# Spilled split weight parts, nine operand pages and x chunks in other tiles, in a decoder trunk on one core

## The chip, the core and the metric

The kernel runs on one core of a Trainium2 chip. The metric is the device time of one execution in microseconds (us), the median of several runs. The engines named below are PE (TensorE, the matrix products; PEld are its weight loads), ACT (ScalarE), DVE (VectorE), POOL (GpSimd) and SP (SyncE, which issues nearly all DMA transfers here).

## The reference, cut to what matters

One layer over 2048 positions of width 1024, in float32. Two mixers share one input product (w_in has 3584 columns, which are 28 blocks of 128): a gated linear recurrence of 1024 channels and a short convolution of 512 channels. Then an output product, a gated feed-forward with a convolution, and norms.

```
h = rms_norm(x, norm1_g[l])
z = jnp.einsum('bsd,de->bse', h, w_in[l])
lru_x, lru_gate, sc_b, sc_c, sc_x = jnp.split(z, splits, axis=-1)
lru_x = causal_dwconv(lru_x, lru_conv_w[l]) + lru_conv_b[l]
y_lru = rg_lru(lru_x, lru_wa[l], lru_ba[l], lru_wx[l], lru_bx[l], lru_lambda[l]) \
    * jax.nn.gelu(lru_gate)
y_sc = sc_b * causal_dwconv(sc_c * sc_x, sc_conv_w[l])
y_mix = jnp.concatenate([y_lru, y_sc], axis=-1)
x = x + jnp.einsum('bse,ed->bsd', y_mix, w_out[l])
h = rms_norm(x, norm2_g[l])
u = causal_dwconv(jnp.einsum('bsd,df->bsf', h, w_up[l]), ffn_conv_w[l])
gate, up = jnp.split(u, 2, axis=-1)
x = x + jnp.einsum('bsf,fd->bsd', jax.nn.gelu(gate) * up, w_down[l])
return rms_norm(x, final_g)
```

`rg_lru` forms r and i = sigmoid of two block-diagonal products (the gates), a = exp(-8 r softplus(-lambda)), and scans h[t] = a h[t-1] + sqrt(1 - a^2) i x.

## The kernel before

**Arithmetic.** x is held as its transpose: 8 chunks of 128 partitions by positions. Each float32 operand is split in two: ACT copies it rounded ("hi", L214), DVE subtracts to get the rest ("lo", L215). A product is then three matmuls: hi by hi, hi by lo, lo by hi. A name wh_ or xh is a hi part, wl_ or xl (as an operand) a lo part.

**Stages.** Positions go in two halves of 1024. The first half's input product (0 to 524 us of the profiled execution) takes the 28 blocks one by one, in the order 0, 8, 1, 9, 20, 24, 21, 25, 16, 17, 2, 10, 3, 11, 4, 12, 5, 13, 6, 14, 7, 15, 22, 26, 23, 27, 18, 19; a block is 48 matmuls of 128x512 (L277). Blocks c and 8 + c make recurrent unit c (the input and its gate), 16 to 27 the short convolution. Beside the products runs the tail of each unit: evacuation of PSUM, convolution (L336, L338), the split of its result (xch, xcl) as the operand of the gate products (L373), eight sigmoids (L384), Exp, Tanh, Square and Sqrt (L389 to L393), the scan (L397), Gelu (L400), and the stores of y. Then come the output product's sweeps of that half (524 to 640 us, L967), the second half's input product (640 to 1010 us, L673), its sweeps (to 1176 us), and the feed-forward's up and down products of both halves (to the end).

**The second half.** Its input product goes by pairs of blocks: 14 pairs, each a 2 by 2 problem done in seven products (Strassen-Winograd) of 12 matmuls. Its weight operands are the quarters W11 and W12 (halves of block a of the pair), W22 (of block b), and the sums S1 to S4 of quarters. S1 to S3 are added by DVE in the first half (`pair_sums`, L261) and spilled to DRAM (`si_d`); in the second half `in_weights` (L808) loads two raw tiles for a pair, splits seven operands and adds S4. The steps of a pair are: `begin` (W11), `middle` (S2, then W12 between, then S3), `fourth` (W22), `sum1` (S1) and `end` (S4). The name zxin is the PSUM tile that W11, S2, S3 and W22 add up in one after the other; ACT copies it out in between (L684): g0, g1 to one tile (xlin, prin or sbin), n1 and n0 to another (soin). The tail of the recurrent pair before stands in the step behind `fourth`.

**What sets the order.** PE, SP and POOL run in the order in which the code is written. ACT and DVE are ordered by a scheduler, by the priorities the code gives (weight splits have a raised one) and by when it reckons operands ready. Each engine runs its row in order. SP's row is strict: a transfer that waits for a tile holds all behind it. `defer(n, ...)` notes a store, and `tick()`, called once for each block, issues it n calls later.

**Tiles.** The pools are: "act", 28 pages of 4 KB a partition; "tmp", 7 pages; "w" and "v", 5 each (weights' hi and lo, in turn); "wr", 4 raw weight tiles; "a" and "b" of the pool `ub`, two wide tiles each (`big`). A load into a tile waits for the last reader of what was there. In the first half the eight x chunks of the second half (`xs`, loaded by L1039) are squared on the way for the second half's norm, one after each unit; they take "act" pages, which the tails use as well.

Of the kernel before, what the change touches and what calls it, by code (L numbers as in the profile page):

```python
# [60 lines left out]
}  # L61
PAIR_OF = {o: (PAIRS.index(p), i) for p, ab in BLOCKS.items() for i, o in enumerate(ab)}

TERMS = [("W11", "B11"), ("S2", "T2"), ("S3", "T3"), ("W22", "T4"), ("S1", "T1"), ("S4", "B22"), ("W12", "B21")]

SUMS = [("S1", "W21", "W22"), ("S3", "W21", "W11"), ("S2", "W11", "S1"), ("S4", "W12", "S2")]

# [12 lines left out]
def block_kernel(  # L80
# [44 lines left out]
    si_d = [dr.tile([P, 3, NB], F32, name=f"si_d{i}") for i in range(len(PAIRS))]  # L125
# [117 lines left out]

    raw_of = {}

    def load_weights(o, name, gate=None):
        tick()
        raw_of[o] = raw_tile(f"wr_{name}")
        out = next(load_parts(w_in[o], name, 1, gate, raw_of[o]))
        i, _ = PAIR_OF[o]  # L250
# [124 lines left out]

    def lru_scan(c, half, cv, g, *gates, home=None, sign=1.0):
        n = f"{half}_{c}"
        r, i = (flat((home or act)(f"{x}{n}")) for x in "ri")
        a = big(f"a{n}", c % 2)[:, :T] if home else flat(act(f"a{n}"))
        with tc.high_priority(offset=HP):  # L380
            for k, (rows, ps) in enumerate(zip(HALVES, gates)):
                for b, p in enumerate(ps):
                    for dst, o, at in ((r, O_BA, k), (i, O_BX, 1 - k)):
                        nc.scalar.activation(  # L384
                            dst[rows, blk(b)], p[HALVES[at], :], AF.Sigmoid, bias=col(o + c)[rows, :]
                        )
        nc.vector.tensor_tensor(i, i, cv, ALU.mult)
        m = cv
        nc.scalar.activation(a, r, AF.Exp, scale=nc8[:, c : c + 1])  # L389
        nc.scalar.activation(m, r, AF.Tanh, scale=c8[:, c : c + 1])  # L390
# [6 lines left out]
        nc.vector.tensor_tensor_scan(h, a, i, init, ALU.mult, ALU.add)  # L397
# [4 lines left out]
        nc.vector.tensor_tensor(y, g, h, ALU.mult)  # L402
        return y
# [77 lines left out]
    def in_phase(half, acc, between):  # L481
# [22 lines left out]
            x_square(half, k, acc, xs[k])  # L504
        for _ in loads[2]:
            pass
        for c in range(2):
            load_gate(c, raws[2 * c])
        parts = mean_split(acc, f"a{half}")
# [91 lines left out]
    def x1_prep(k, rs):  # L601
        return operands(f"x_{k}", k, lambda kk: xT[kk, :, T:S], O_G1, rs)

    def operands(name, k, src, gain, rs):
        a = big(f"ha{name}", 0)[:, :T]
        b = big(f"hb{name}", 0)[:, :T]
# [55 lines left out]
    class Pair:  # L662
# [27 lines left out]
        def spread(self):  # L690
            self.open()
            ps = {w: pst(f"z{w}{self.name}") for w, _ in TERMS}
            for k in range(4):
                for w, x in TERMS:
                    self.run(ps[w], w, x, True, True, (k,))
            (g0, g1), (n0, n1) = self.g, self.n
            self.x = ps["W11"]
            self.copy(g0)
# [10 lines left out]
                    nc.vector.tensor_tensor(dst, ps[w], src, ALU.add)  # L709
            self.second_done()  # L710
            self.first_done()

        def begin(self):
            self.open()
# [13 lines left out]
        def middle(self, between):  # L728
            self.run(self.x, "S2", "T2", False, False)
            self.copy(self.g[1])  # L730
            between()
            self.run(self.x, "S3", "T3", False, False)
            self.copy(self.n[1])
            self.add(self.n[1], self.c)

# [70 lines left out]
            cur = nxt  # L806
            between(j)

    def in_weights(i):
        a, b = BLOCKS[PAIRS[i]]  # L810
        one, other = raw_tile(f"wra_in{i}"), raw_tile(f"wrb_in{i}")
        nc.sync.dma_start(one[:, 0, :], w_in[a][:, :NB])
        nc.sync.dma_start(one[:, 1:3, :], si_d[i][:, 1:3, :])
        nc.sync.dma_start(other[:, 0, :], w_in[a][:, NB:])
        nc.sync.dma_start(other[:, 1, :], w_in[b][:, NB:])
        nc.sync.dma_start(other[:, 2, :], si_d[i][:, 0, :])
        tick()
        out = {}

        def operand(name, src):  # L820
            w = page(f"w{name}_in{i}", "v" if i == 0 and name in ("W22", "S4") else "w", 5)
            split(w[:, 0, :], w[:, 1, :], src)
            out[name] = (w[:, 0, :], w[:, 1, :])

        operand("W11", one[:, 0, :])
        operand("S1", one[:, 1, :])
        operand("S2", one[:, 2, :])
        nc.vector.tensor_tensor(one[:, 2, :], one[:, 2, :], other[:, 0, :], ALU.add)
        operand("W12", other[:, 0, :])
        operand("S3", other[:, 2, :])  # L830
        operand("W22", other[:, 1, :])
        operand("S4", one[:, 2, :])
        return out

    def vpage(name):
        return page(name, "v", 5)
# [1 line left out]
    class InPair(Pair):  # L838
# [5 lines left out]
        def open(self):  # L844
# [5 lines left out]
                self.first = with_halo(f"pr{n}", 2, 1, p_halo[:, c, :], c % 2, nc.vector)  # L850
                self.g = halves(self.first, 2)
            else:
                self.first = flat(tmp(f"sb{n}"))
# [10 lines left out]
    def in_blocks(hs, start):  # L864
        half = 1
        gates = {}
        sv = {}
        wts = [in_weights(0), in_weights(1)]
        state = {"gw": None}

        def load_gates(q):
# [4 lines left out]
        def finish(pair):  # L876
            n = UNITS.index(("L" if pair.kind == "L" else "S", pair.unit))
            if pair.kind == "L":
                c = pair.unit
                xc, cv = lru_conv_of(c, half, pair.first, vpage)  # L880

                def gated():
                    if c % 4 == 0:
                        load_gates(c // 4)
                    g = state["gw"][:, c % 4, :]
                    return lru_gates(c, half, xc, (g[:, :P], g[:, P:]))

                def scanned(pss):
                    y = lru_scan(c, half, cv, pair.other, *pss, home=tmp, sign=-1.0)
                    keep_y(half, n, y, (1, 1))  # L890

                gates[pair.name] = (gated, scanned)
# [14 lines left out]
        cur = InPair(0, hs, wts[0])  # L907
        last = None
        for j in range(len(PAIRS)):
            if j + 2 < len(PAIRS):  # L910
                wts.append(in_weights(j + 2))
            else:
                tick()
            nxt = InPair(j + 1, hs, wts[j + 1]) if j + 1 < len(PAIRS) else None
            if j == 0:
                cur.spread()
                nxt.begin()
            elif nxt is None:
                cur.middle(cur.sum1)
                cur.second()  # L920
                cur.fourth()
            else:
                cur.middle(cur.second)
                nxt.begin()
# [6 lines left out]
            if nxt is not None and j + 2 < len(PAIRS):  # L931
                nxt.sum1()
            if j > 0:
                cur.end()
# [92 lines left out]
    def beside_first(n):  # L1027
# [7 lines left out]
                nc.scalar.activation(t, t, AF.Square)  # L1035
                nc.vector.tensor_tensor(ss1[1], ss1[1], t, ALU.add)
        if n < KC:
            t = x1_raw[n] = flat(act(f"xs{n}"))
            nc.sync.dma_start(t, xT[n, :, T:S])  # L1039
# [258 lines left out]
```

## Time and profile before

| what | us |
|---|---|
| median of 3 runs (lowest, highest) | 2548.32 (2544.07, 2548.89) |
| the profiled execution, its own time | 2548.74 |
| its span in the trace | 2545.9 |
| PE busy, share of the span | 2275.8, 89% |
| DVE busy | 1812.3, 71% |
| ACT busy | 1233.6, 48% |
| first half's input product | 0 to 524 |
| sweeps, first half | 524 to 640 |
| second half's input product | 640 to 1010 |

The profiled execution stands at the median of the runs. What lies around its span is 2.84 us. The page's section 2 shows the span in 40 slices of 63.6 us, with the busy tenths of each engine, the granted TensorE clock and the DMA rate:

```profile
PE   8676547799989677899999999999999999999998
PEclk9787868899999889899999999999999999999999
GB/s 186 168 137 57 62 116 126 45 320 284 186 161 186 153 145 97 278 270 91 116 108 88 118 106 87 269 213 222 238 112 87 118 106 87 121 105 300 280 193 179
```

PE is under nine tenths busy in the first eight slices and in slices 12 to 16, and its clock is lower there.

### The profile page before, as it was taken

The numbers are of one execution on the slowest core, as the hardware profiler recorded it, in microseconds if no ns is written. First come the engines' busy times: TensorE is split into PE (matmuls) and PEld (weight loads), VectorE is DVE, ScalarE is ACT, GpSimd is POOL, SyncE is SP. The second block draws the span as 40 slices with busy tenths as digits, with TensorE's granted clock in tenths as the row PEclk, the third lists the DMA queues.
The fourth block names the chain that finished last, engine by engine and source line by source line (L and its number), as shares of the span: only waits on it lengthen the run. The fifth ranks groups of instructions, "written<-read, shape, count | busy, mean of one in ns | idle before, by whom it ended". The sixth has DMA issues, their size and how long they took to land.

```text
span 2545.9 us, 26290 instructions
## 1 busy us (share of the span) xinstructions
PE 2275.8 (89%) x9814; PEld 1854.2 (73%) x9814; DVE 1812.3 (71%) x2108; ACT 1233.6 (48%) x1427; POOL 136.2 (5%) x187
## 2 busy tenths in 40 slices
PE   8676547799989677899999999999999999999998
PEld 6455436678767555677888888888888888888886
DVE  8444436589676556698888788867788788787656
ACT  6513345245656765354554454544445454444343
POOL 0000000000000000000111111000001001000000
PEclk9787868899999889899999999999999999999999
DMA  6551133198656553772332332766632332338765
GB/s 186 168 137 57 62 116 126 45 320 284 186 161 186 153 145 97 278 270 91 116 108 88 118 106 87 269 213 222 238 112 87 118 106 87 121 105 300 280 193 179
DMA packets 160048, 402.41 MB, mean 158 GB/s; under 512 B 15472, under 2 KB 19184, under 8 KB 159344
## 3 DMA queue, kind: packets, MB, share of 16 engines
q1 hardware_dynamic: 149984, 381.86, 43.5%
q0 software_dynamic: 9792, 18.88, 4.6%
q8 instruction: 76, 1.25, 0.2%
q14 instruction: 52, 0.43, 0.1%
q10 hardware_dynamic: 144, 0.00, 0.0%
HBM read 301.07 MB, written 137.36 MB: 172 GB/s over the span
## 4 chain that ended last, share of the span: by engine, by line
PE 76%; DVE 10%; ACT 8%; issue 3%; DMA 2%; SPq 0%; DVEq 0%; ACTq 0%
PE zx L673 20%; PE zin_b L277 11%; PE zc L673 10%; PE dx L967 10%; PE dy L967 8%; PE za L673 5%; PE ox L967 4%; PE zxin L673 4%; PE oy L967 2%; DVE cv L338 2%; ACT r L384 1%; ACT i L384 1%; PE zcin L673 1%; PE zS L673 1%; DVE r L397 1%
## 5 line engine op out<-in xcount | busy, mean ns | idle before, releaser
L277 PE MATMUL zin_b<-xh,wh_in 128*128 128x512 f32 x448 | 148.8, 415 | 145.9 <-ACT wh_in L214 145.9
L277 PEld LDWEIGHTS zin_b<-xh,wh_in 128*128 128x128 f32 x448 | 89.6, 202 | 169.2 <-ACT wh_in L214 149.7
L215 DVE TENSOR_TENSOR fl_d<-wrf_d,fh_d 128x1024 fp32r<-128x1024 f32 x84 | 102.8, 1223 | 123.0 <-ACT fh_d L214 120.5
L214 ACT ACTIVATE fh_d<-wrf_d 128x1024 fp32r<-128x1024 f32 x84 | 89.0, 1060 | 206.2 <-PE dy L967 84.7
L277 PE MATMUL zin_b<-xh,wl_in 128*128 128x512 f32 x448 | 146.2, 409 | 11.6 <-DVE wl_in L215 11.6
L215 DVE TENSOR_TENSOR wla_up<-wra_up,wha_up 128x1024 fp32r<-128x1024 f32 x48 | 58.8, 1225 | 132.8 <-ACT wha_up L214 132.8
L967 PE MATMUL dx<-fh_d,wh_d 128*128 128x512 f32 x384 | 149.4, 389 | 0.0
L967 PE MATMUL dx<-fl_d,wh_d 128*128 128x512 f32 x384 | 149.4, 389 | 0.0
L967 PE MATMUL dx<-fh_d,wl_d 128*128 128x512 f32 x384 | 149.4, 389 | 0.0
L277 PE MATMUL zin_b<-xl,wh_in 128*128 128x512 f32 x448 | 146.1, 408 | 0.2
L338 DVE SCALAR_TENSOR_TENSOR cu<-un,prm,cu 128x1024 f32<-128x1024 f32 x96 | 122.6, 1277 | 4.4 <-ACT cu L334 4.3
L338 DVE SCALAR_TENSOR_TENSOR cg<-ug,prm,cg 128x1024 f32<-128x1024 f32 x96 | 122.7, 1278 | 0.3
L673 PE MATMUL zc<-hhB,whd_up 128*128 128x512 f32 x368 | 120.7, 389 | 0.0
L673 PE MATMUL zx<-ht,whc_up 128*128 128x512 f32 x368 | 113.3, 389 | 0.0
L277 PEld LDWEIGHTS zin_b<-xh,wl_in 128*128 128x128 f32 x448 | 88.1, 198 | 34.1 <-DVE wl_in L215 15.6
L967 PE MATMUL dy<-fh_d,wh_d 128*128 128x512 f32 x288 | 112.0, 389 | 0.0
L967 PE MATMUL dy<-fl_d,wh_d 128*128 128x512 f32 x288 | 112.0, 389 | 0.0
L967 PE MATMUL dy<-fh_d,wl_d 128*128 128x512 f32 x288 | 112.0, 389 | 0.0
L684 ACT ACTIVATE ug<-zx 128x512 f32<-128x512 f32 x92 | 55.0, 598 | 114.8 <-PE zx L673 114.7
L215 DVE TENSOR_TENSOR wl_d<-wrw_d,wh_d 128x1024 fp32r<-128x1024 f32 x84 | 102.3, 1219 | 11.3 <-ACT wh_d L214 10.0
L277 PEld LDWEIGHTS zin_b<-xl,wh_in 128*128 128x128 f32 x448 | 89.2, 200 | 21.0 <-DVE xl L460 1.4
L214 ACT ACTIVATE wh_d<-wrw_d 128x1024 fp32r<-128x1024 f32 x84 | 88.0, 1048 | 22.2 <-DMA wrw_d<-sd_d_S 7.4
(439 smaller groups left out, 6393.5 us busy)
## 6 DMA issues: line engine op xcount, KB each, us to landing
wra_up<-in_w_up SPq DMA_DIRECT2D x48, 512.0 KB, 4.6
wrb_up<-in_w_up SPq DMA_DIRECT2D x48, 512.0 KB, 5.3
f_d_T<-cg SPq DMA_DIRECT2D x96, 256.0 KB, 2.5
wrw_d<-sd_d_S SPq DMA_DIRECT2D x48, 512.0 KB, 4.5
wrf_d<-f_d_T SPq DMA_DIRECT2D x48, 512.0 KB, 4.2
f_d_B<-cu SPq DMA_DIRECT2D x72, 256.0 KB, 2.4
wrw_d<-in_w_down SPq DMA_DIRECT2D x36, 512.0 KB, 4.6
wrf_d<-f_d_B SPq DMA_DIRECT2D x36, 512.0 KB, 3.4
```

The source lines that it names most:

```text
L214: nc.scalar.activation(r32(hi), src, AF.Copy)
L215: nc.vector.tensor_tensor(r32(lo), src, hi, ALU.subtract)
L277: nc.tensor.matmul(ps[t], r32(a), r32(b[:, blk(t)]), start=(first and i == 0), stop=(last and i == 2))
L338: nc.vector.scalar_tensor_tensor(dst, src[:, k : k + T], col(o_w + k), dst, ALU.mult, ALU.add)
L384: nc.scalar.activation(dst[rows, blk(b)], p[HALVES[at], :], AF.Sigmoid, bias=col(o + c)[rows, :])
L397: nc.vector.tensor_tensor_scan(h, a, i, init, ALU.mult, ALU.add)
L673: nc.tensor.matmul(ps, r32(p[:, s]), r32(self.hs[k][x][o]), start=f and i == 0, stop=l and i == 2, skip_group_check=True,)
L684: nc.scalar.activation(dst, self.x, AF.Copy)
L967: nc.tensor.matmul(ps[m], r32(p), r32(x[:, k, :]), start=first and i == 0 and n == 0, stop=(last or not on_x) and i == ni - 1 and n == 2, ...
```

## The change

There are three parts.

- *Spilling.* In the first half `keep_weights` stores hi and lo of W11, W12 and W22 to a new DRAM tile `sw_d`, two ticks after the block's split; `pair_sums` also adds S4, and `si_d` has room for it. SP has 997 rows instead of 913.
- *The second half.* `in_weight` loads one operand at a time: W11, W12, W22 from `sw_d` into a "w" page, without a split; S1 to S4 from `si_d` into a raw tile that is split in place. Nine operands are loaded up front, then seven a step in the order of their use. The stores that are due (`tick`) now go ahead of a step's loads. The tile `so` is taken later (`open_second`), `sb` and the scan's r come from "v" pages, and gate weights are loaded when a pair is finished. The last pair runs like the others.
- *x chunks.* `xs` takes a wide tile of side n % 2 instead of an "act" page, and the first operand of the residual (`x1_prep(0, ...)`) has its second tile on side "b".

```diff
-TERMS = [("W11", "B11"), ("S2", "T2"), ("S3", "T3"), ("W22", "T4"), ("S1", "T1"), ("S4", "B22"), ("W12", "B21")]
+TERMS = [("W11", "B11"), ("S1", "T1"), ("S2", "T2"), ("S3", "T3"), ("W22", "T4"), ("S4", "B22"), ("W12", "B21")]
...
+    def keep_weights(o, hl):
+        i, b = PAIR_OF[o]
+        for n, t in enumerate(hl):
+            t = t.rearrange("p (a b) -> p a b", a=2)
+            if b:
+                defer(2, sw_d[i][:, 2, n, :], t[:, 1, :])
+            else:
+                defer(2, sw_d[i][:, 0:2, n, :], t)
...
+                (ra, 1, ra[:, 1, :], ra[:, 0, :]),
...
-        defer(2, si_d[i][:, 2, :], ra[:, 0, :])
+        defer(2, si_d[i][:, 2:4, :], ra[:, 0:2, :])
...
-        r, i = (flat((home or act)(f"{x}{n}")) for x in "ri")
+        r, i = (flat(p(f"{x}{n}")) for p, x in zip(home or (act, act), "ri"))
...
+    def in_weight(i, op):
+        n = f"w{op}_in{i}"
+        if op in KEPT:
+            t = page(n, "w", 5)
+            nc.sync.dma_start(t, sw_d[i][:, KEPT.index(op)])
+            return t[:, 0, :], t[:, 1, :]
+        t = raw_tile(n)
+        nc.sync.dma_start(t[:, 2, :], si_d[i][:, SPILLED.index(op), :])
+        split(t[:, 0, :], t[:, 1, :], t[:, 2, :])
+        return t[:, 0, :], t[:, 1, :]
...
-            self.other = flat(tmp(f"so{n}"))
+
+        def open_second(self):
+            self.other = flat(tmp(f"so{self.name}"))
...
-        wts = [in_weights(0), in_weights(1)]
+        load(*((0, w) for w, _ in TERMS), (1, "W11"), (1, "S1"))
...
-            if j + 2 < len(PAIRS):
-                wts.append(in_weights(j + 2))
-            else:
-                tick()
+            tick()
+            load(
+                (j + 1, "S2"),
+                (j + 1, "W12"),
+                (j + 1, "S3"),
+                (j + 2, "W11"),
+                (j + 1, "W22"),
+                (j + 2, "S1"),
+                (j + 1, "S4"),
+            )
...
-            t = x1_raw[n] = flat(act(f"xs{n}"))
+            t = x1_raw[n] = big(f"xs{n}", n % 2)[:, :T]
...
-            hx.append(x1_prep(0, ss1[1]))
+            hx.append(x1_prep(0, ss1[1], 1))
```

How the rows of the engines move, at three places. First ACT in the first half, at unit 3 (r_3, a_3, cv_3 are its gate, decay and root; wh_in_12, wh_in_5, wh_in_13 and wh_in_6 are the hi copies of these blocks). Before:

```order
L389 ACTIVATE a_3_1649<-r_3_1647,nc_81 128x1024
L390 ACTIVATE cv_3_1452<-r_3_1647,c_80 128x1024
L1035 ACTIVATE xs_1675<-xs_1675 128x1024
L391 ACTIVATE r_3_1647<-a_3_1649 128x1024
L393 ACT_TABLE_LOAD
L393 ACTIVATE cv_3_1452<-cv_3_1452 128x1024
L214 ACTIVATE wh_in_12_1685<-wr_in_12_1684 128x1024
L214 ACTIVATE wh_in_5_1748<-wr_in_5_1747 128x1024
```

And after:

```order
L217 ACTIVATE wh_in_12_1734<-wr_in_12_1733 128x1024
L217 ACTIVATE wh_in_5_1800<-wr_in_5_1799 128x1024
L403 ACT_TABLE_LOAD
L403 ACTIVATE a_3_1696<-r_3_1694,nc_81 128x1024
L404 ACTIVATE cv_3_1494<-r_3_1694,c_80 128x1024
L1054 ACTIVATE xs_1913<-xs_1913 128x1024
L405 ACTIVATE r_3_1694<-a_3_1696 128x1024
L407 ACT_TABLE_LOAD
L407 ACTIVATE cv_3_1494<-cv_3_1494 128x1024
L414 ACT_TABLE_LOAD
L414 ACTIVATE g_4_1792<-g_4_1792 128x1024
L217 ACTIVATE gw_5_1806<-wr_in_5_1799 128x128
```

The split of block 12 moved from behind the root of unit 3 to ahead of its exponential. In the rows that follow, the split of block 13 moved from behind the root of unit 4 to ahead of that unit's sigmoids.

The second place is ACT at the first unit, where block 20's split stood. Before, it was behind the whole tail of unit 0 (eight sigmoids, which are r_0 and i_0, are left out here); the piece from the last of the tail on is:

```order
L389 ACTIVATE a_0_736<-r_0_734,nc_81 128x1024
L390 ACTIVATE cv_0_595<-r_0_734,c_80 128x1024
L400 ACT_TABLE_LOAD
L400 ACTIVATE g_1_731<-g_1_731 128x1024
L391 ACTIVATE r_0_734<-a_0_736 128x1024
L393 ACT_TABLE_LOAD
L393 ACTIVATE cv_0_595<-cv_0_595 128x1024
L214 ACTIVATE wh_in_20_766<-wr_in_20_765 128x1024
```

And after, ahead of the sigmoids:

```order
L414 ACTIVATE g_0_651<-g_0_651 128x1024
L217 ACTIVATE wh_in_20_788<-wr_in_20_787 128x1024
L217 ACTIVATE xch_1_743<-cv_1_738 128x1024
L1054 ACTIVATE xs_886<-xs_886 128x1024
L398 ACT_TABLE_LOAD
L398 ACTIVATE r_0_750<-zr_0_b_717,prm 64x512
```

The split moved past the whole tail of unit 0.

The third place is SP's row in the second half, at one step (wra_in and wrb_in are raw weight tiles, wS_in and wW_in operands, y_d the stores of y, yc and soin the results of a unit's tail). Before:

```order
L812 DMA wra_in_4955<-in_w_in 128x512
L813 DMA wra_in_4955<-si_d_258 128x1024
L814 DMA wrb_in_4956<-in_w_in 128x512
L815 DMA wrb_in_4956<-in_w_in 128x512
L816 DMA wrb_in_4956<-si_d_258 128x512
L211 DMA y_d_B_1_109<-soin_4563 128x512
L211 DMA y_d_T_1_118<-yc_4_4914 128x512
```

And after:

```order
L214 DMA y_d_B_1_109<-soin_4717 128x512
L214 DMA y_d_T_1_118<-yc_4_4918 128x512
L837 DMA wS_in_4961<-si_d_257 128x512
L834 DMA wW_in_4965<-sw_d_271 128x1024
L837 DMA wS_in_4967<-si_d_257 128x512
L834 DMA wW_in_4971<-sw_d_272 128x1024
L834 DMA wW_in_4973<-sw_d_271 128x1024
L837 DMA wS_in_4975<-si_d_258 128x512
L837 DMA wS_in_4979<-si_d_257 128x512
```

The stores of y moved from behind a step's loads to ahead of them, and five loads became seven.

More of the change, by code (lines that the diff above doesn't have):

```diff
@@ L62 @@
 PAIR_OF = {o: (PAIRS.index(p), i) for p, ab in BLOCKS.items() for i, o in enumerate(ab)}
[L64 removed]
+TERMS = [("W11", "B11"), ("S1", "T1"), ("S2", "T2"), ("S3", "T3"), ("W22", "T4"), ("S4", "B22"), ("W12", "B21")]
+KEPT = ["W11", "W12", "W22"]
+SPILLED = ["S3", "S1", "S2", "S4"]
 SUMS = [("S1", "W21", "W22"), ("S3", "W21", "W11"), ("S2", "W11", "S1"), ("S4", "W12", "S2")]
@@ L124, in block_kernel @@
     sd_d = blocks("sd_d", S_OPS, NI)
-    si_d = [dr.tile([P, 3, NB], F32, name=f"si_d{i}") for i in range(len(PAIRS))]
+    si_d = [dr.tile([P, 4, NB], F32, name=f"si_d{i}") for i in range(len(PAIRS))]
+    sw_d = [dr.tile([P, 3, 2, NB], F32, name=f"sw_d{i}") for i in range(len(PAIRS))]
     sg_d = dr.tile([2, P, NLRU // 2, 2 * P], F32, name="sg_d")
@@ L249, in load_weights @@
         out = next(load_parts(w_in[o], name, 1, gate, raw_of[o]))
+        keep_weights(o, out)
         i, _ = PAIR_OF[o]
@@ L506, in in_phase @@
             pass
+        for o, w in zip((0, NLRU, 1), wts):
+            keep_weights(o, w)
         for c in range(2):
@@ L599, in h_prep, with x1_prep, operands @@
         return operands(f"{half}_{k}", k, lambda kk: x2_d[half][kk // 2][kk % 2], O_G2, rs)
-    def x1_prep(k, rs):
-        return operands(f"x_{k}", k, lambda kk: xT[kk, :, T:S], O_G1, rs)
-    def operands(name, k, src, gain, rs):
+    def x1_prep(k, rs, side=0):
+        return operands(f"x_{k}", k, lambda kk: xT[kk, :, T:S], O_G1, rs, side)
+    def operands(name, k, src, gain, rs, side=0):
         a = big(f"ha{name}", 0)[:, :T]
-        b = big(f"hb{name}", 0)[:, :T]
+        b = big(f"hb{name}", side)[:, :T]
         for t, kk in ((a, k), (b, k + 4)):
@@ L695, in spread @@
                     self.run(ps[w], w, x, True, True, (k,))
+            self.open_second()
             (g0, g1), (n0, n1) = self.g, self.n
@@ L711, in spread @@
             self.first_done()
+        def open_second(self):
+            pass
         def begin(self):
@@ L732, in middle @@
             self.run(self.x, "S3", "T3", False, False)
+            self.open_second()
             self.copy(self.n[1])
@@ L807, in up_phase @@
             between(j)
[L809 to L816, printed above, removed]
-        tick()
[L818 to L833, printed above, removed]
+    def in_weight(i, op):
[8 more added lines that the diff above has]
+        return t[:, 0, :], t[:, 1, :]
     def vpage(name):
@@ L852, in open, with open_second @@
             else:
-                self.first = flat(tmp(f"sb{n}"))
+                self.first = flat(vpage(f"sb{n}"))
                 self.g = halves(self.first, 0)
-            self.other = flat(tmp(f"so{n}"))
+        def open_second(self):
+            self.other = flat(tmp(f"so{self.name}"))
             self.n = halves(self.other, 0)
@@ L867, in in_blocks, with load @@
         sv = {}
-        wts = [in_weights(0), in_weights(1)]
+        wts = [{} for _ in PAIRS]
+        def load(*which):
+            for i, op in which:
+                if i < len(PAIRS):
+                    wts[i][op] = in_weight(i, op)
+        load(*((0, w) for w, _ in TERMS), (1, "W11"), (1, "S1"))
         state = {"gw": None}
@@ L880, in finish @@
                 xc, cv = lru_conv_of(c, half, pair.first, vpage)
+                if c % 4 == 0:
+                    load_gates(c // 4)
                 def gated():
-                    if c % 4 == 0:
-                        load_gates(c // 4)
                     g = state["gw"][:, c % 4, :]
@@ L888, in scanned @@
                 def scanned(pss):
-                    y = lru_scan(c, half, cv, pair.other, *pss, home=tmp, sign=-1.0)
+                    y = lru_scan(c, half, cv, pair.other, *pss, home=(vpage, tmp), sign=-1.0)
                     keep_y(half, n, y, (1, 1))
@@ L917, in in_blocks @@
                 nxt.begin()
[L918 to L921, printed above, removed]
             else:
                 cur.middle(cur.second)
-                nxt.begin()
+                if nxt is not None:
+                    nxt.begin()
                 cur.fourth()
@@ L930, in in_blocks @@
                 last = None
-            if nxt is not None and j + 2 < len(PAIRS):
+            if nxt is not None:
                 nxt.sum1()
```

1 line of the change is left out of this document (removed).

## The prediction

> **What bounds the kernel now.** I read the busy time per stage first (one row is a stretch: length, then busy time and instructions of PE, PEld, DVE, ACT and POOL, the granted TensorE clock, DMA share, GB/s), then PE's waits, the single stalls, ACT's row of work ahead of one, SP's waits, and the DMA rows.
>
> ```profile
> core 0: us, PE busy (x) PEld busy (x) DVE busy (x) ACT busy (x) POOL busy (x), PEclk, DMA share, GB/s
> 74.00:181.00 107.00, 84.50 (x347) 68.44 (x348) 51.08 (x61) 25.90 (x28) 7.17 (x8) 0.85 0.64 182
> 181.00:524.00 343.00, 217.36 (x897) 171.45 (x896) 172.65 (x198) 144.63 (x155) 0.90 (x1) 0.79 0.26 87
> 524.00:640.00 116.00, 114.38 (x505) 94.37 (x504) 106.66 (x125) 57.96 (x62) 0.00 (x0) 1.00 0.88 303
> 640.00:1040.00 400.00, 322.58 (x1330) 253.06 (x1329) 250.49 (x304) 244.97 (x319) 21.43 (x24) 0.91 0.57 166
> 1040.00:2546.00 1506.00, 1484.72 (x6515) 1225.52 (x6514) 1177.92 (x1326) 708.75 (x801) 102.91 (x144) 0.99 0.46 159
> ```
>
> From 524 to 640 us and from 1040 us on PE is busy without holes; 114.38/505 gives 0.2265 us a matmul at full clock. The change touches nothing of weight there, and I leave these stages as they are. What can be won lies in the two product stages, 0 to 524 and 640 to 1040. No engine is full in them, so it is a chain of waits that sets the time.
>
> ```profile
> PE zin_b L277 <- ACT wh_in L214: 145.9, 9, 21.8
> PE zin_b L277 <- DVE wl_in L215: 11.6, 4, 7.5
> PE ms_a L309 <- ACT rh_a L214: 9.6, 2, 9.3
> ...
> SPq L1039 <- PE zr_b L373: 111.1, 3, 43.0
> ...
> SPq L1039 <- PE zi_b L373: 39.9, 1, 39.9
> SPq L1039 <- DVE r L397: 33.6, 1, 33.6
> SPq L1039 <- DVE xcl L215: 26.3, 1, 26.3
> ```
>
> Up to 530 us PE stands 145.9 us for the hi copy of a weight block, nine times. The SP rows say what is late ahead of that: L1039 loads an x chunk into an "act" page, and waits 111.1 + 39.9 + 33.6 + 26.3 = 211 us for a page that the gates or the scan still hold. The weight loads stand behind it in SP's row.
>
> ```profile
> 74.87 1.22 PE L277 MATMUL zin_b<-xh,wh_in 128*128 128x512 f32 x2 [20.12 <-ACT wh_in L214]
> ...
> 103.12 1.22 PE L277 MATMUL zin_b<-xh,wh_in 128*128 128x512 f32 x2 [14.13 <-ACT wh_in L214]
> ...
> 190.88 0.79 PE L277 MATMUL zin_b<-xh,wh_in 128*128 128x512 f32 x1 [9.43 <-ACT wh_in L214]
> ...
> 239.46 1.22 PE L277 MATMUL zin_b<-xh,wh_in 128*128 128x512 f32 x2 [21.70 <-ACT wh_in L214]
> ...
> 287.48 0.79 PE L277 MATMUL zin_b<-xh,wh_in 128*128 128x512 f32 x1 [21.77 <-ACT wh_in L214]
> ...
> 335.63 1.22 PE L277 MATMUL zin_b<-xh,wh_in 128*128 128x512 f32 x2 [21.82 <-ACT wh_in L214]
> ...
> 388.58 0.80 PE L277 MATMUL zin_b<-xh,wh_in 128*128 128x512 f32 x1 [21.70 <-ACT wh_in L214]
> ...
> 510.02 1.22 PE L277 MATMUL zin_b<-xh,wh_in 128*128 128x512 f32 x2 [14.78 <-ACT wh_in L214]
> ```
>
> These are blocks 20, 24, 10, 11, 12, 13, 14 and 19 of the input weights, in the order of the program. Next comes ACT ahead of the stall of block 11, and what PE loses behind two stalls:
>
> ```profile
> 222.60 1.06 ACT L214 ACTIVATE xch<-cv 128x1024 fp32r<-128x1024 f32 x1 [4.05 <-DVE cv L338]
> 223.67 1.28 ACT L384 ACT_TABLE_LOAD   x1
> 224.97 0.68 ACT L384 ACTIVATE r<-zr_b,prm 64x512 f32<-64x512 f32 x1
> ...
> 231.85 1.15 ACT L389 ACTIVATE a<-r,nc 128x1024 f32<-128x1024 f32 x1
> 232.90 1.13 ACT L390 ACTIVATE cv<-r,c 128x1024 f32<-128x1024 f32 x1
> 233.94 1.04 ACT L1035 ACTIVATE xs<-xs 128x1024 f32<-128x1024 f32 x1
> ...
> 238.37 1.99 ACT L214 ACTIVATE wh_in<-wr_in 128x1024 fp32r<-128x1024 f32 x2
> ...
> 74.87 12.53 PE zin_b L277 x48
> ...
> 239.46 24.45 PE zin_b L277 x95
> ```
>
> ACT runs the whole tail of one recurrent unit, 222.60 to 238.37, and only then the split for which PE stands. Behind a stall 48 matmuls take 12.53 us where 48 x 0.2265 = 10.87 would do, and 95 take 24.45 against 21.5: 1.7 to 2.9 us lost to a low clock for each long stall.
>
> **The change, part by part.** *The x chunks in the big tiles.* They no longer wait for pages; the 211 us of SP's wait go, and the weight loads come early. In the order of the changed program the splits of blocks 20, 24, 10, 11, 13, 15 and 19 stand ahead of the unit's tail on ACT, not behind it; 12 stands behind the sigmoids, 14 behind sigmoids and exponential. That gives, stall by stall:
> - Block 20 jumps gate copy, table load, eight sigmoids and the rest, about 16 to 20 us of ACT's work; of 20.1 I take 18 (bounds 15 and 20.1).
> - Block 24 jumps unit 1's tail: 13 of 14.1 (10 to 14.1). Block 21's lo wait (7.5 in the row of wl_in) loses about 4.7 (0 to 7.5), since its load comes before a shorter tail.
> - Blocks 10, 11, 13, 19: 9.4, 21.7, 21.8 and 14.8, all of it, since the split is a tail earlier than PE (together 67.7; 45 if a late load gives a third of it back).
> - Block 12 now stands ahead of the exponential, tanh, squares and root (some 7 us by the rows above), but PE arrives earlier too and then waits for the unit's gates: 3 (0 to 7.7). Block 14: 1 (0 to 7). The wait of ms_a: 1 (0 to 9).
>
> The sum is 18 + 13 + 4.7 + 67.7 + 5 = 108. Six of the long stalls go, each with 1.7 to 2.9 us of low clock: 6 x 2.2 = 13. The first half ends 121 us earlier, with the bounds at about 80 and 143. What is late next there: blocks 12 and 14 still stand some 20 us each.
>
> A rule of the Trainium skill bears on the clock term. "TensorE: Matmul & The Clock Gate", section "What's actually happening", says that the clock is halved after an idle window of about 3.4 us and whole again after about 3.4 us of work. By it a stall costs an estimated 1.7 us more, six cost 10 and the sum would be 118; the rows of 12.53 us agree with it, those of 24.45 us say more, and I keep the rows.
>
> *The added stores.* Each of 28 blocks stores hi and lo: 14 times 2 x 512 KB and 14 times 2 x 256 KB, with the fourth sum 14 x 256 KB, about 25 MB. They go through SP, 84 issues, and each stands ahead of loads if its split isn't done; it is given two ticks of delay.
>
> ```profile
> DMA packets 26874, 63.29 MB, mean 119 GB/s; under 512 B 2863, under 2 KB 6575, under 8 KB 26662
> ...
> wr_in<-in_w_in SPq DMA_DIRECT2D x25, 512.0 KB, 5.3
> ```
>
> Up to 530 us 63.29 MB are moved; 88 MB in some 400 us is 220 GB/s, where the trace shows 303 at a share of 0.88 in the stage 524 to 640. So it fits, and I cost the stores at nothing; the cover is a load's lead of one block, 48 x 0.2265 = 10.9 us, against 5.3 to land. If it is gone each block starts late by a part of 5.3 us: 0 to 60 us in all, kept for a rival. The Trainium skill, "DMA: Bandwidth & Descriptors", section "Specifications", gives about 358 GB/s as a core's share of HBM; by it the stores would be hidden as well. The 14 further adds of the fourth sum are 14 x 0.69 (a 128x512 operation of DVE, in a row below) = 10 us, on an engine that is busy in half of that stage: nothing.
>
> *The second half.* PE's waits, ACT's copy and DVE's work behind it, a stretch of one recurrent pair, a split's price on ACT, and a load:
>
> ```profile
> PE zxin L673 <- ACT soin L684: 51.2, 8, 10.0
> ...
> PE zr_b L373 <- DMA gp<-sg_d: 3.9, 1, 3.9
> ...
> 856.24 0.60 ACT L684 ACTIVATE soin<-zxin 128x512 f32<-128x512 f32 x1 [4.08 <-DVE r L397]
> ...
> 856.24 1.23 DVE L402 TENSOR_TENSOR soin<-soin,r 128x1024 f32<-128x1024 f32 x1
> 857.50 0.69 DVE L563 TENSOR_TENSOR yd<-soin,soin 128x512 f32<-128x512 f32 x1
> ...
> 857.00:895.00 38.00, 25.03 (x96) 19.29 (x96) 21.12 (x24) 23.97 (x30) 1.79 (x2) 0.81 0.50 145
> ...
> L214 ACT ACTIVATE wW_in<-wrb_in 128x512 fp32r<-128x512 f32 x27 | 16.8, 622 | 13.8 <-issue 5.0 <-PE zxin L673 3.1 <-PE zcin L673 2.4
> ...
> wrb_in<-si_d SPq DMA_DIRECT2D x14, 256.0 KB, 5.7
> ```
>
> PE stands 51.2 us, in 8 stalls, for a copy out of PSUM whose tile the scan of the unit before still holds (856.24, released by the scan). The new order of tiles frees the copy, gate weights load earlier (3.9), and three splits fewer a pair take 14 x 3 x 0.62 = 26 us off ACT. But the loads now stand on SP behind the y stores, and these wait for the same scan. S2 of the next pair then is there a product (1.2), a combination (0.7 to 2), a landing (5.7) and a split (1.3) after the scan, 9 to 10 us; PE has about four runs of 12 matmuls to do meanwhile, 48 x 0.2265 = 10.9. So the wait moves from the copy to S2 and comes out nearly even: I take -5. One bound is -35 (all of the 51.2 and 3.9 and 8 x 2 of low clock is 71; ACT's own 24 us a step stay, which leave half), the other +20 to 30 (a landing later by 2.5 to 4 us in eight pairs). Bytes for a pair grow from 1.5 to 2.5 MB: 14 MB in 400 us add 36 to the 166 GB/s, well under 303.
>
> *Nothing else:* hb of the first x operand moved to the other tile, gains no time; the order of terms in the one pair that is spread changes no count of matmuls.
>
> **The rivals.** A. The second half recovers as well: if the stores leave SP before the next step's loads are needed, its loss of 51.2 goes down to what ACT bounds: -35, so 2548.7 - 121 - 35 = 2393. For it: ACT has 26 us less; against it: the order of SP puts loads behind y. B. The stores crowd SP: every block's load stands behind a store that waits for the lo split; some 22 blocks then are late by about 2.8 us each, which gives 60 back: 2548.7 - 121 + 60 - 5 = 2483. For it: SP's row is served in order; against it: a mean of 220 GB/s and two ticks of delay. C, slower: in the second half the S2 load comes late in every one of 13 steps, by more than 121/13 = 9.3 us each; from there the kernel is slower; at 10.5 us it is 2564. Against it: the load needs 5.7 us, and PE's own work covers 10.9. D. No effect: ACT takes the splits in the old order because loads still come late, and all stays within 0.2%, about 5 us, which is also what a measurement of this kernel can tell from no change. Against it: the tiles of the x chunks are free long before.
>
> **How the numbers follow.** The profiled execution took 2548.74 us, the median is 2548.32: no difference. 2548.74 - 121 - 5 = 2422. Chances: this forecast 0.66 (its own range 2395 to 2460), A 0.13, B 0.15, C 0.04, D 0.02. The range takes A and B in: 2383 (a little beyond A) to 2483. Faster holds this, A and B: 0.94; same D: 0.02; slower C: 0.04.
>
> **What would show it.** Right: in the changed profile the first sweep begins near 403 us instead of 524; PE's wait for wh_in falls from 145.9 to about 45, left at blocks 12 and 14; SP's waits of the x chunk loads are gone; in the second half the wait for the copy of soin is nearly gone, and a wait for an S2 split or its load stands in its place; the stage lasts about 395 us. Wrong: if PE waits for wl or wh of other blocks with the stores' DMA or SP ahead of it (B), if the second half lasts under 370 us (A), or if x chunk loads still wait (D).

## The result, and the profile after

The changed kernel takes 2441.24 us (median of 4 runs, 2439.4 to 2443.81) against 2547.9 us before: ratio 0.9585, 95% interval 0.9568 to 0.9601. The profiled execution took 2440.47 us, its span is 2438.7 us. One execution far apart from its kernel's other three (3268.47 us against 2380.29 to 2383.88, of the kernel with the later preparation below) is in none of the ratios.

Stage by stage (from one stage's first matmul on PE to the next one's, and at the end of the second half's product to its last; in the two profiled executions):

| stage | before, us | after, us | difference | forecast |
|---|---|---|---|---|
| first half's product | 523.6 | 401.5 | -122.1 | -121 |
| first output sweeps | 120.3 | 129.5 | +9.2 | 0 |
| second half's product | 365.8 | 374.5 | +8.7 | -5 |
| second sweeps | 166.1 | 164.6 | -1.5 | 0 |
| the feed-forward, to the end | 1370.1 | 1368.6 | -1.5 | 0 |

The prediction's "about 395 us" for the second half counts from 640 to 1040 us and so takes in 30 us of sweeps; by the bounds of this table it stands for some 361 us. Its sign of rival A, under 370 us, means nothing by these bounds, since the kernel before took 365.8.

The same view of busy time per stage after the change, at its own stage ends (from 60 us on, the columns as before):

```profile
60.00:183.00 123.00, 116.03 (x499) 94.26 (x500) 86.28 (x118) 60.79 (x65) 8.97 (x10) 0.95 0.91 286
183.00:401.50 218.50, 170.43 (x744) 137.22 (x743) 145.43 (x170) 124.30 (x133) 0.00 (x0) 0.88 0.44 157
401.50:531.00 129.50, 121.37 (x509) 98.67 (x508) 109.15 (x126) 60.73 (x64) 0.00 (x0) 0.95 0.80 282
531.00:906.00 375.00, 313.36 (x1274) 243.28 (x1272) 199.47 (x232) 211.20 (x267) 21.47 (x24) 0.92 0.66 193
906.00:2438.00 1532.00, 1501.56 (x6568) 1238.43 (x6568) 1196.77 (x1346) 720.32 (x812) 104.31 (x144) 0.99 0.48 163
```

PE's matmuls are the same. Over the first half's product, before and after:

```profile
0.00:523.60 523.60, 353.72 (x1466) 280.93 (x1467) 276.83 (x356) 221.90 (x247) 11.83 (x19) 0.82 0.38 117
...
0.00:401.50 401.50, 339.88 (x1467) 274.46 (x1468) 279.33 (x365) 219.46 (x243) 11.85 (x19) 0.92 0.63 209
```

So 108 us of idle time went, and 13.8 us of busy time: the same matmuls ran at a mean granted clock of 0.92 instead of 0.82. The sweeps, which ran at 1.00, now show 0.95: there are new holes. PE's waits up to 460 us, and the rows of SP up to 401 us that wait longest:

```profile
PE zin_b L291 <- ACT wh_in L217: 46.1, 4, 21.5
PE ms_a L323 <- ACT rh_a L217: 8.3, 1, 8.3
PE zin_b L291 <- DVE wl_in L218: 5.7, 1, 5.7
PE ox L986 <- ACT fh_o L217: 4.4, 1, 4.4
...
SPq L214 <- DVE gw L218: 111.9, 7, 37.3
SPq L214 <- DVE sv L459: 42.9, 1, 42.9
...
SPq L1058 <- ACT ss_a L1052: 6.2, 1, 6.2
```

145.9 us have become 46.1. The load of an x chunk (now L1058) no longer waits for gates or a scan; what remains of its 211 us is 6.2. Instead SP's longest waits are stores: of gate weights (gw) and of one y (sv). The stalls that are left, as PE's single instructions:

```profile
61.32 1.22 PE L291 MATMUL zin_b<-xh,wh_in 128*128 128x512 f32 x2 [6.05 <-ACT wh_in L217]
...
93.55 0.80 PE L291 MATMUL zin_b<-xh,wl_in 128*128 128x512 f32 x1 [5.65 <-DVE wl_in L218]
...
215.19 1.22 PE L291 MATMUL zin_b<-xh,wh_in 128*128 128x512 f32 x2 [18.21 <-ACT wh_in L217]
...
285.59 0.80 PE L291 MATMUL zin_b<-xh,wh_in 128*128 128x512 f32 x1 [21.48 <-ACT wh_in L217]
```

They are blocks 20, 21, 12 and 14. In the second half's product, PE's and ACT's waits:

```profile
PE zxin L689 <- ACT soin L700: 22.2, 8, 4.8
PE zxin L689 <- ACT prin L700: 15.6, 4, 5.9
PE zxin L689 <- ACT xlin L700: 10.6, 3, 6.9
PE zxin L689 <- ACT wS_in L217: 8.3, 3, 3.5
...
ACT wS_in L217 <- DMA wS_in<-si_d: 73.1, 20, 9.2
```

The wait for the copy of soin fell from 51.2 to 22.2 us, but ACT now stands 73.1 us for loads of the sums, with the copies of prin and xlin behind them (4.8 and 4.0 us of PE's waits before). All of PE's waits in this stage come to 64.4 us in 14 stalls before and to 61.3 us in 22 after. The busy time is what grew:

```profile
643.90:1009.70 365.80, 301.27 (x1264) 238.15 (x1263) 227.28 (x275) 230.76 (x303) 21.43 (x24) 0.92 0.54 150
...
531.00:905.50 374.50, 313.00 (x1274) 243.28 (x1272) 199.37 (x231) 211.20 (x267) 21.47 (x24) 0.92 0.66 192
```

Ten matmul records more account for some 2 us of the 11.7. The granted clock is 0.92 in both, so it doesn't tell why the rest of the matmuls took longer; matmuls behind the stalls that grew did (those of zxin that the waits for prin and xlin stand ahead of: 420 ns in the mean before, 476 after), while those behind the copies of soin got faster (492 and 457).

### The profile page after: what moved, and what is told of

Its sections match the earlier page's. It is cut to its first block, busy times and chain, and to the rows that moved or that the text cites. A ratio compares the mean times of both kernels' runs of the same rounds, so it can differ in the third digit from the quotient of the medians.

```text
span 2438.7 us, 26314 instructions
## 1 busy us (share of the span) xinstructions
PE 2276.2 (93%) x9814; PEld 1854.8 (76%) x9814; DVE 1784.7 (73%) x2066; ACT 1211.7 (50%) x1385; POOL 137.6 (6%) x187
## 4 chain that ended last, share of the span: by engine, by line
PE 72%; DVE 10%; ACT 9%; DMA 5%; issue 2%; SPq 1%; DVEq 0%; ACTq 0%
PE zx L689 21%; PE dx L986 11%; PE zc L689 10%; PE dy L986 8%; PE zin_b L291 6%; PE za L689 5%; PE ox L986 3%; PE oy L986 3%; PE zxin L689 2%; DMA wS_in<-si_d 2%; ACT r L398 2%; ACT i L398 2%; DVE cv L352 1%; DVE r L411 1%; PE zS L689 1%
## 5 line engine op out<-in xcount | busy, mean ns | idle before, releaser
L291 PE MATMUL zin_b<-xh,wh_in 128*128 128x512 f32 x448 | 144.3, 404 | 46.1 <-ACT wh_in L217 46.1
L689 PE MATMUL zc<-hhB,whd_up 128*128 128x512 f32 x368 | 120.8, 389 | 0.0
```

The costliest lines, as they stand in the source:

```text
L291: nc.tensor.matmul(ps[t], r32(a), r32(b[:, blk(t)]), start=(first and i == 0), stop=(last and i == 2))
L689: nc.tensor.matmul(ps, r32(p[:, s]), r32(self.hs[k][x][o]), start=f and i == 0, stop=l and i == 2, skip_group_check=True,)
```

## The experiments

The theory at the start: the tiles of the x chunks alone make the first half's gain; the spilled parts and the loads make the second half and the sweeps longer. "The two lines" below are the tile of the x chunks and the side of hb, which every run moved together. Ratios are to the kernel before, run beside each; stage lengths are from the profiled execution.

**Only the wide tiles** (the kernel before, with `xs` and `x1_prep` of the change):

```diff
-            t = x1_raw[n] = flat(act(f"xs{n}"))
+            t = x1_raw[n] = big(f"xs{n}", n % 2)[:, :T]
```

> The kernel before with only the x chunks in the wide tiles; no spilled parts, old second half. Theory (the tiles alone make the first half's gain, and the added stores make the first output sweep 9 us longer): the first half's product ends near 401 us, the sweep takes 120 us as before, the second half's product 366 us, the time is about 2426 us. Rival (the sweep is longer because DVE carries work over from a product stage that ends sooner): the sweep takes about 129 us here too, the time is about 2435 us. If the spilled parts were what moves the splits, the time stays near 2548 us.

Measured: 2416.09 us, ratio 0.9491 (0.9477 to 0.9505), 25 us faster than the whole change. The first half's product ends at 385.3 us, the sweeps take 129.8, the second half's product 366.1. So the two lines give the first half's gain and 16 us more; the sweeps are longer without any spilled store, as the rival said (its reason, work that DVE carries over, falls below); the second half's loss isn't there. PE's waits in the first half:

```profile
PE zin_b L277 <- ACT wh_in L214: 39.3, 3, 20.1
PE ms_a L309 <- ACT rh_a L214: 8.5, 1, 8.5
```

Blocks 12 and 14 are the 39.3; the stalls at 20 and 21 are absent.

**The change without the wide tiles** (the two lines as before):

> The changed kernel with the x chunks back in act pages. Theory: the long stalls come back, the first half's product lasts 520 to 530 us, the second half stays 9 us worse, the time is 2550 to 2565 us. Rival (spilling and the order of loads have a part in the gain): the time is under 2520 us.

Measured: 2572.65 us, ratio 1.0108 (1.0091 to 1.0125): the rest of the change by itself is 1.1% slower. The first half's product takes 538.7 us, 15.1 more than before, the second half's 380.4, 14.6 more; these and the time lie above what was expected. The sweeps take 123.2 us, so most of their growth went with the two lines. The x chunk's load waits again:

```profile
SPq L1058 <- PE zr_b L387: 109.3, 3, 41.7
...
SPq L1058 <- PE zi_b L387: 40.9, 1, 40.9
```

**The loads ahead of the y stores** (`tick()` moved behind the loads of a step in the second half):

```diff
-            tick()
             load(
...
             )
+            tick()
```

> The changed kernel with the y stores issued behind a step's loads in the second half, as before the change. Theory (the loads behind the y stores cost the second half what the freed copy gave): the second half's product takes 345 to 360 us instead of 374, the time is 2415 to 2430 us. Rival (the loads wait anyway, for tiles that PE still reads): within 5 us of 2441 us.

Measured: 2440.5 us, ratio 0.9596 (0.9578 to 0.9614): no change. The profiled execution took 2449.0 us, so its second half's product of 383.6 us overstates the length by up to 9. The wait only changed its name:

```profile
SPq L837 <- PE zcin L689: 179.0, 24, 19.2
...
ACT wS_in L217 <- DMA wS_in<-si_d: 75.0, 31, 6.5
```

A raw tile holds the operand too, since it is split in place, and SP waits 179 us (68.2 before this edit) until PE has read one. With the y store out of the way that wait ends last. The theory that y alone delays the loads fell.

**S2 in a page of its own as well** (that edit, and S2 of pairs 1 to 13 in a tmp page):

```diff
+        if op == "S2" and i:
+            t = tmp(n)
+            nc.sync.dma_start(t[:, 1, :], si_d[i][:, SPILLED.index(op), :])
+            split(t[:, 0, :], t[:, 1, :], t[:, 1, :])
+            return t[:, 0, :], t[:, 1, :]
```

> The changed kernel with the y stores behind the loads and operand S2 of pairs 1 to 13 in a tmp page of its own (split in place), so that its load waits neither for y nor for a raw tile that PE reads. Theory (the loss of the second half is operands that come late because a raw tile is the operand too and stays taken until PE has read it): ACT's wait for loads of si_d falls from 73 us to under 40 us, the second half's product takes 350 to 362 us, the time is 2417 to 2429 us. Rival (ACT's tail of a unit is the bound): within 5 us of 2441 us.

Measured: 2431.26 us, ratio 0.9551 (0.9535 to 0.9567), 10 us less than the change; the second half's product takes 364.4 us. The direction is the theory's, but all three of its numbers missed, the time and the stage by 2 us and the wait of ACT by far, 66.8 us and not under 40:

```profile
ACT wS_in L217 <- DMA wS_in<-si_d: 66.8, 25, 6.0
```

S1, S3 and S4 still share four tiles, of which each is taken from the issue of its load to PE's last read.

**The gate weights' stores later:**

```diff
-        defer(1, sg_d[c // 4, :, c % 4, :], gw[:, : 2 * P])
+        defer(5, sg_d[c // 4, :, c % 4, :], gw[:, : 2 * P])
```

> The changed kernel with the stores of the gate weights issued five blocks after they are noted, not one. Theory (the two stalls of about 20 us that are left, at blocks 12 and 14, come from a store of gate weights that holds SP, with these blocks' loads behind it): both stalls shrink to under 5 us, the time is 2400 to 2412 us. Rival (ACT's own row sets the splits): the stalls stay, within 5 us of 2441 us.

Measured: 2395.78 us, ratio 0.9416 (0.9402 to 0.943), 45 us faster than the change from one digit. SP waited 111.9 us for gw, up to 37.3 at once, with the loads of blocks 12 and 14 behind it; now the rows of SP and PE are:

```profile
PE zin_b L291 <- ACT wh_in L217: 1.6, 2, 1.2
...
SPq L214 <- DVE gw L218: 3.1, 2, 1.6
```

The first half's product ends at 356.2 us. The stalls at blocks 20 and 21 went with it. So the stalls at blocks 12 and 14 lay in SP's row, and not in ACT's.

**The first stores later** (`keep_weights` of blocks 0, 8 and 1 with five ticks and not two):

> The changed kernel with the first three blocks' split parts stored five blocks after they are noted, not two. Theory (the stalls of 6 us at block 20 and of 5.7 us at block 21, which the kernel with only the wide tiles doesn't have, come from these stores ahead of the loads on SP): the stall at block 20 goes, the first half's product ends near 393 us instead of 401, the time is about 2433 us. Rival (DMA bandwidth, not SP's row): the stalls only move, within 5 us of 2441 us.

Measured: 2436.74 us, ratio 0.9568 (0.9554 to 0.9582), overlapping the change's; in the profile the first half's product ends at 396.3 us, 5.2 earlier, and neither stall is there. In part they moved, as the rival said: a stall of 3.9 us stands at block 25, the one behind 21, instead, the one at block 12 grew from 18.2 to 19.9 us, and PE's wait for wh_in is 45.6 us against 46.1. The time moved 4.5 us, half of what was forecast and within the rival's range. What held block 20's load is in SP's row of the changed kernel:

```profile
SPq L240 <- DMA si_d<-wr: 10.5, 1, 10.5
```

The load waits for a raw tile whose own store, put behind six stores of split parts, hasn't landed yet; before the change this row was 6.9 us, and with the first stores later it is 6.7.

**Wide tiles and late gate stores, nothing spilled:**

> The kernel before with the x chunks in the wide tiles and the gate-weight stores five blocks late; nothing spilled, old second half. Theory (the two gains add, the spilled parts are no part of either): first half's product ends near 341 us (385 less the 39 us of stalls at blocks 12 and 14 and 2 x 2 us of low clock), time about 2372 us. Rival (without the spilled stores SP waits elsewhere): 2385 us or more.

Measured: 2388.6 us, ratio 0.9382 (0.9368 to 0.9396). The stalls for wh_in are gone (0.4 us), but the first half's product ends at 356.1, not 341, and the time is in the rival's range: with PE ahead, ms_a waits 11.3 us and the gate products 5.1 us for PSUM that sigmoids still read, and PE is busy 336.4 us where the kernel with only the wide tiles has 333.6. Sweeps (132.8) and second half (369.7) came out 3 to 4 us longer than in the kernel with only the wide tiles. Where the gate stores are late, the spilled stores cost the first half nothing: 356.2 with them, at a DMA share of 0.96 from 60 to 183 us, and 356.1 without.

**The tile moves too** (that kernel, with `open_second`, sb and r in v pages and the early gate load of the change; loads and splits as before):

```diff
-        r, i = (flat((home or act)(f"{x}{n}")) for x in "ri")
+        r, i = (flat(p(f"{x}{n}")) for p, x in zip(home or (act, act), "ri"))
...
-            self.other = flat(tmp(f"so{n}"))
+        def open_second(self):
+            self.other = flat(tmp(f"so{self.name}"))
```

> As e5_xs_late_gates, and in the second half the tile moves of the change alone (so taken late, sb and r in v pages, gate weights loaded early), with the old loads and splits. Theory (these moves free the copies that wait for the scan, and nothing else makes the second half longer): the second half's product takes 335 to 355 us instead of 366, the time is 2340 to 2362 us. Rival (the tail of the unit sets the steps whatever the tiles): within 5 us of e5_xs_late_gates.

Measured: 2377.26 us, ratio 0.9334 (0.932 to 0.9348), 11 us less than without the moves. The second half's product takes 358.4 us, 11.3 less; both missed what was expected, 335 to 355 us and 2340 to 2362 us. This kernel and the one with late gate stores and the whole change differ in the spilled parts and single loads alone: 358.4 against 372.4 us in that stage, 2377.26 against 2395.78 in time. So the tile moves give 11 us and the single loads, with the order of operands that goes with them, take 14 back: PE's waits differ by 3 us of it (55.3 and 58.4), its busy time by 10.8 (303.1 and 313.9). PE's and ACT's first rows with the tile moves:

```profile
PE zxin L673 <- ACT soin L684: 39.3, 8, 8.8
...
ACT wS_in L214 <- PE zxin L673: 51.7, 20, 5.6
```

Here ACT's split of a sum waits for an operand page that PE reads, and not for a load. The wait for the copy of soin is 39.3 us, with the old tiles it was 49.8, so the moves free a fifth of it; the wait for the gate weights' load, 6.2 us there, is gone.

**The longer sweeps: the operand's preparation later, and earlier** (on that kernel):

> As e8_tiles, with the preparation of the first second-half operand moved from the last units of the first half into the first output sweep (beside steps 1, 4, 8 and 14 instead of unit 10 and steps 3, 8 and 14). Theory (the first sweep is 9 us longer because DVE comes to it with this preparation still to do, ahead of the splits of the sweep's own operands): PE's waits for fh_o and fl_o at the start of the sweep, 3.6 us on ox, go, the sweep takes 121 to 126 us instead of 130, the time is 2368 to 2374 us. Rival (DVE is as short of time inside the sweep, or the sweep's loads are late whatever DVE does): the waits move to later steps and the sweep stays at 128 us or more.

> As e8_tiles, with the same preparation one unit earlier (beside unit 9). Theory: some of it is done before the first half's last blocks end, the sweep takes 125 to 129 us instead of 130, the time is 2372 to 2377 us. Rival (the order of DVE's rows at the start of the sweep hardly changes, so nothing does): within 3 us of e8_tiles.

Measured: later, ratio 0.9355 (0.934 to 0.9371), the sweeps 135.0 us, with PE's wait at their start up from 2.8 to 7.1:

```profile
PE ox L975 <- ACT fh_o L214: 7.1, 1, 7.1
```

Earlier: 2376.61 us, ratio 0.9334 (0.9319 to 0.935), the sweeps 130.4, nothing changed, though the operand's last split ended at 337 us, 18 us ahead of the sweeps. DVE's work carried over isn't the cause; that theory fell twice.

**The last y store one step later** (on that kernel again):

```diff
-            keep_y(half, n, y, (2, 8) if n >= NOUT - 2 else (7, 7))
+            keep_y(half, n, y, (3, 8) if n >= NOUT - 2 else (7, 7))
```

> As e8_tiles, with the stores of the last even short-convolution unit's y (B11 and T1) issued one step later, behind the loads of the first sweep's second step and not ahead of them. Theory (the first sweep is longer because this store holds SP until the unit's sv is ready, some 43 us, and the loads of the second step then come in a burst about 5 us ahead of PE instead of 10): PE's waits at the start of the sweep go, it takes 120 to 125 us instead of 130, the time is 2367 to 2373 us. Rival (the DMA rings are the bound of the sweep's start, whoever is first): the sweep stays at 128 us or more, the time within 3 us of e8_tiles.

Measured: 2374.26 us, ratio 0.9331 (0.9315 to 0.9346), against 0.9334: within the interval, so by its time alone it shows nothing, and both numbers of the theory were just missed. The stage shows it: 125.5 us instead of 130.4, and PE's wait for fh_o on ox is gone. SP's queue says why, first the changed kernel around the start of its sweeps (401.5 us), then this one (354.0 us):

```profile
352.22 0.46 SPq L214 DMA_DIRECT2D sw_d<-wl_in  x1
395.64 0.33 SPq L214 DMA_DIRECT2D y_d_B<-sv  x1
396.36 0.33 SPq L214 DMA_DIRECT2D y_d_T<-yc  x1
396.79 0.40 SPq L999 DMA_DIRECT2D wrw_o<-in_w_out  x1
```

```profile
326.90 0.33 SPq L988 DMA_DIRECT2D wrw_o<-in_w_out  x1
327.99 0.33 SPq L988 DMA_DIRECT2D wrf_o<-y_d_B  x1
...
349.28 0.32 SPq L211 DMA_DIRECT2D y_d_B<-sv  x1
350.01 0.32 SPq L211 DMA_DIRECT2D y_d_T<-yc  x1
```

In the changed kernel the loads of the second step were issued at 396.79, 4.7 us before the sweeps began; here at 326.90, 27 us before. With the tile moves alone, which is what this edit starts from, it was 4.3 us. The lead goes with the stage's length in the other kernels too: 10 us in the kernel before (120.3 us), 9 in the change without the wide tiles (123.2), 4.7 with only the wide tiles (129.8). So the loads' lead explains 4.9 of the 10.1 us. Of the 5.2 that are left, 3 are busy time (120.8 us instead of 117.8, at a granted clock of 0.97 instead of 1.00) and 2 idle; 3.8 us of waits stay on ox and oy, 1.6 before, and no run takes those away.

## Why the prediction was right, and where not

- *The x chunks in the wide tiles.* That the two lines take the stalls away is shown (with and without them, in two kernels); the runs don't part SP's shorter waits from the new order of ACT's row. PE's waits in the first half fell by 108.0 us (145.9 + 11.6 + 9.6 + 1.5 to 46.1 + 5.7 + 8.3 + 0.5), forecast 108. That the stage came out at -122.1 for -121 is luck in part: by themselves the two lines gave -138.3, some 17 more than forecast, and the stores, forecast at nothing, took 16.2 back. Blocks 20 and 21 kept 6.05 and 5.65 us, where about 2 and 2.8 were forecast.
- *Blocks 12 and 14.* They stayed as forecast, 18.21 and 21.48 us, but not for the reason given, ACT's tail and the unit's gates: with the gate stores later both were gone. A store on SP held their loads.
- *Block 19.* Its 14.8 us went as forecast, again for another reason than an x chunk's wait and ACT's tail. The rows of the kernel before show what held it:

```profile
SPq L608 <- DVE sv L338: 77.0, 1, 77.0
...
498.92 0.33 SPq L608 DMA_DIRECT2D hbx<-in_xT  x1
...
501.90 1.39 SPq L237 DMA_DIRECT2D wr_in<-in_w_in  x1
...
506.07 1.06 ACT L214 ACTIVATE hhB11x<-hax 128x1024 fp32r<-128x1024 f32 x1 [38.85 <-DVE hax L615]
...
508.93 1.04 ACT L214 ACTIVATE wh_in<-wr_in 128x1024 fp32r<-128x1024 f32 x1
```

SP stood 77.0 us at the load of hb (hbx), and block 19's load came behind it; on ACT, block 19's split stood behind that operand's. Moving hb to the other tile, which the prediction put at no gain, is what took this wait away. With both lines back it is 63.1 us, and block 19's stall 15.8; no run moves hb alone.
- *The clock term.* Six long stalls and 13.8 us of busy time make 2.3 us each, forecast 2.2. The Trainium skill, "TensorE: Matmul & The Clock Gate", section "What's actually happening", gives an estimated 1.7 by its two windows of 3.4 us; the measurement is a third above it, with what shorter stalls cost in it.
- *The added stores at nothing.* This step failed. They cost 16 us in the first half as the kernel stands (385.3 to 401.5), and 15.1 with the x chunks in pages. It isn't the bytes, since with the gate stores moved the same bytes cost nothing (356.2 and 356.1); it is the order on SP. One such place is shown, a raw tile that its store gives back later and the next load waits for, and it is worth some 5 of the 16 us. The Trainium skill, "DMA: Bandwidth & Descriptors", section "Specifications", names about 358 GB/s as a core's share of HBM; by it too they would be hidden, so a rate doesn't tell what a queue costs. (Slices of this trace lie above that figure, at some 400 GB/s; see the end.)
- *The second half at -5.* The sign was wrong. PE's waits did come out nearly even, 64.4 to 61.3 us, as the step said, and the wait moved to late loads and the copies behind them. The loads are late not only behind y, which was all that the step had, but because a raw tile stays taken as the operand. What the step left out is that 22 shorter stalls in place of 14 go with 11.7 us more of busy time. In parts: the tile moves are worth -11, and the single loads +14.
- *The sweeps at nothing.* This term was missed, +9.2. In the kernel before, SP stood at the load of hb; the y store of sv behind it then found sv ready, and the loads of the second step left 10 us ahead of the sweeps. In the changed kernel SP stands 42.9 us at that y store instead, and they leave 4.7 us ahead. The 77.0 us stood in the trace of before, and the prediction didn't ask what would come last once they were gone. Half of the growth is shown to hang on this; the other half stays open.
- *The rivals.* B's price (some 60 us) didn't come, but its mechanism did, at a quarter of the size. A's -35 didn't come; the tile moves alone reach a third of it. C and D didn't come.

## What to carry to other kernels

Read the in-order DMA queue as an engine: a store that waits for its operand holds every load behind it, and moving the store by a few steps gave 45 us here, four times what the tile moves of the second half gave. When a stall goes, ask what was done during it; the next stage's loads may have lived on it. A buffer that is load target and operand in one is taken from issue to last read, so the number of such buffers is the lead of the loads. Spilling a split took time off ACT here (230.8 to 211.2 us busy in the second half's product) and still made the kernel slower (by 18 us, between the two kernels with the tile moves and late gate stores), with the loads late.

## What the runs showed of the hardware

The DMA rate of short stretches lies well above the means of the stages (303 GB/s in the sweeps before, 282 after). Around the start of the sweeps, first the kernel before (507 to 560 us), then the changed one (385 to 440 us):

```profile
GB/s 216 254 289 379 102 49 312 155 209 393 397 413 403 318 263 312 400 405 419 410 397 403 403 405 411 396 405 403 396 243 303 207 278 189 220 136 292 402 390 280
...
GB/s 0 0 0 0 0 0 0 0 229 232 203 295 399 405 402 399 425 302 410 407 405 404 419 386 390 405 410 414 399 392 413 399 350 54 7 220 161 149 232 244
```

Each figure is a slice of 1.3 or 1.4 us; where the rings are busy, most lie about 400 GB/s in both kernels. A 512 KB load there takes 5.6 to 9.6 us to land before and 6.8 to 10.4 after (medians by tile), against 5.3 for the weight blocks of the first half before. The zeros ahead are SP, held by a store.
